# Two matmuls instead of three per weight tile in the SwiGLUs of a hybrid encoder trunk, in groups of eight, and 1/rms of their norm later

## The chip, the cores and the metric

One core of one Trainium2 chip runs the whole program in one launch. The metric is the device time of an execution in microseconds; the figure of a kernel is the median of its runs.

## The reference, cut to what is computed

Two layers over 256 tokens of width 1024 in float32, each with two SwiGLU half-steps around a mixer, then a gated per-layer input:

```python
for i in range(DEPTH):                                   # 2
    x = x + 0.5 * swiglu(rmsnorm(x, g_ffa[i]), ...)      # silu(h @ w_gate) * (h @ w_up) @ w_down, 1024 -> 2816 -> 1024
    u = rmsnorm(x, g_mix[i]) @ w_in[i]                   # neighbourhood attention and Hyena convolution on its columns
    ...
    x = x + 0.5 * swiglu(rmsnorm(x, g_ffb[i]), ...)
    x = x + sigmoid(rmsnorm(x, g_ple[i]) @ w_ple_gate[i]) * (p[i] @ w_ple_proj[i])
return rmsnorm(x, g_final)
```

## The kernel before, in words

Activations lie turned: features on the 128 partitions, the 256 tokens (T) along the row. `x` is eight such blocks. A float32 product is made from rounded parts: every operand is split into a high part (fp32r, the rounded value) and a low part (the rest), and `mm3` (L164) issues three TensorE matmuls for each 128x128 weight tile: high weight on high input (L165), high weight on low input (L166), low weight on high input (L167), all of 256 columns, into the same 256 columns of a PSUM bank. A bank holds 512 float32 per partition, and there are eight (`bank`, L99).

Weights come as a stream of 1 MB pieces of 16 tiles (`load`, L213; three buffers), and are split in halves of 8 tiles by `part` (L234): ScalarE casts the high part (L250), VectorE subtracts for the low part (L253; in the mixer every third one on GpSimd). Six halves are held; when half n is begun, `refill` (L270) lets the split of half n + 5 be issued.

The norm's gain is folded in ahead: `prep` (L327) makes the two parts of g * x (ScalarE L329, VectorE L331), which lie beside one another in one tile of 512 columns, and adds up the squares (ScalarE L314, GpSimd L317). 1/rms is found later by `Rstd` (L365): two small TensorE matmuls per 128 tokens (L379), Newton steps on VectorE, and two matmuls that spread it over all partitions into `rb` (L403 to L405). Its place is set in steps: STAT_F = 8 (STAT0 = 6 in the very first) and SPREAD_AT = 7. The products don't wait for it; the work behind them multiplies by `rb`.

TensorE and ScalarE run in the order in which the program issues their work; the order on VectorE and GpSimd is planned by the framework. The products set the pace: after every three weight tiles (TICK) `tick` lets each live piece of side work ("fiber") issue one step, up to its next `yield`. `finish` makes a fiber issue all that is left before a product that reads its result.

A SwiGLU (`ffn`, L425) first makes four products (gate and up of two blocks of 128 hidden features) together, block of x by block of x, then for each further block of features (22 in all) gate and up into the two halves of one bank. `gated` (L431) multiplies both by `rb` in one VectorE instruction of 512 columns (L439), takes Silu on ScalarE (L442), multiplies (VectorE, L445) and splits the result (L447, L449). The down projection then makes 8 columns of blocks from 22 tiles each, and adds half of each to x (L480). Beside the first SwiGLU of each layer `filter_steps` (L491) computes the Hyena filter's spectrum, on all engines; after the SwiGLUs come the mixer (L611) and the gated input (`ple`).

Of the kernel before, what the change touches and what calls it, by code (L numbers as in the profile page):

```python
# [28 lines left out]
HALF = 8  # L29

# [6 lines left out]
STAT0 = 6  # L37
# [11 lines left out]
SPREAD_AT = 7  # L49
FILTER = 10  # L50
# [9 lines left out]
# columns of the packed per-partition parameters of one layer  # L60
# [15 lines left out]
def hybrid_trunk(ctx: ExitStack, tc: tile.TileContext, w, xT, pT, rpb, small, wf, zT, dft, idft, decay, out):  # L76
# [8 lines left out]
    k1 = ctx.enter_context(tc.tile_pool(name="k1", bufs=12))  # L85
# [33 lines left out]
    class Fiber:  # L119
        """Work of several engines, emitted step by step between the products."""  # L120
# [43 lines left out]
    def mm3(o, lh, ll, rh, rl, start, stop):  # L164
        PE.matmul(o, lh, rh, start=start, stop=False)  # L165
        PE.matmul(o, lh, rl, start=False, stop=False)  # L166
        PE.matmul(o, ll, rh, start=False, stop=stop)  # L167
        if not Pace.inside:
            Pace.total += 1
            Pace.count += o.free_size() // T if hasattr(o, "free_size") else o.shape[-1] // T  # L170
            while Pace.count >= TICK:
                Pace.count -= TICK
                tick()

# [21 lines left out]
    # even times, odd times, and the latter's negative; real and imaginary parts  # L196
# [37 lines left out]
    def part(steps=1):  # L234
        """The next 8 weight tiles in their two 12-bit parts."""
# [25 lines left out]
    def half():  # L261
        """The two parts of the next 8 weight tiles."""
        n = Stream.used
        Stream.used += 1
        h, l, fb = Stream.ready.pop(n)
        fb.finish()
        refill(n - LAG)
        return h, l

    def refill(done):  # L270
        """Halves up to `done` - 1 are used up: others take their place."""
        while Stream.parted < min(done + WBUFS, 2 * DEPTH * PIECES):
            Pace.live.insert(0, part())

    class Tiles:
        """Weight tiles one after the other."""
# [16 lines left out]
    class Inputs:  # L293
        """The two parts of g * x of the norm at hand."""
# [5 lines left out]
        def __getitem__(self, c):  # L300
            hl, fb = self.xs[c]
            fb.finish()
            return hl[:, :T], hl[:, T:]

    class Squares:
        """Sum of the squares of `n` blocks, in whatever order they come."""
# [27 lines left out]
    def onward(i, cg, c, before):  # L334
        """After `before`, which brings x[c] up to date, the next norm's input."""
# [9 lines left out]
    def rsqrt(v):  # L345
        """v ** -0.5 of two columns by Newton's steps from the exponent's halving."""
# [18 lines left out]
    class Rstd:  # L365
        """1/rms of each token: `r`, tokens on partitions, and `dst`, on all partitions."""
# [45 lines left out]
    def norm(xs, at):  # L412
        return Rstd(rb, Norm.sq.parts, D, [fb for _, fb in xs.xs] + early, at)
# [11 lines left out]
    def ffn(i, cg_next, i_next):  # L425
# [3 lines left out]
        rs = norm(xs, STAT0 if Stream.used == 0 else STAT_F)  # L429

        def gated(pg, pu, joint, hl):  # L431
            yield from rest(EV)
            yield from rs.wait()
            gu = t2(s="gu")
            if joint is None:
                V.tensor_mul(gu[:, :T], pg, rb)
                V.tensor_mul(gu[:, T:], pu, rb)
            else:
                V.tensor_tensor(v2(gu), v2(joint), rb2(), op=ALU.mult)  # L439
            yield  # L440
            s = t1()
            S.activation(s, gu[:, :T], AF.Silu)  # L442
            yield
            a = t1()
            V.tensor_mul(a, s, gu[:, T:])  # L445
            yield
            S.copy(hl[:, :T], a)  # L447
            yield
            V.tensor_sub(hl[:, T:], a, f(hl[:, :T]))  # L449

        def start(*a):
            hl = t2(F32R, "act")
            act.append((hl, spawn(gated(*a, hl))))

        heads = [bank()[:, :T] for _ in range(4)]
        for c in range(KD):
            xh, xl = xs[c]
            for o in heads:
                wh, wl = ws.next()
                mm3(o, wh, wl, xh, xl, c == 0, c == KD - 1)  # L460
        for j in (0, 2):
            start(heads[j], heads[j + 1], None)
        for ff in range(2, NF):
            b = bank()
            for o in (b[:, :T], b[:, T:]):
                product(o, ws, xs)
            start(None, None, b)
        ws = Tiles()
        new_norm()
        for c in range(KD):  # L470
            ps = bank()[:, :T]
            for k in range(NF):
                wh, wl = ws.next()
                hl, fb = act[k]
                fb.finish()
                mm3(ps, wh, wl, hl[:, :T], hl[:, T:], k == 0, k == NF - 1)

            def half_step(c=c, ps=ps):
                yield from rest(EV)
                V.scalar_tensor_tensor(x[c], ps, 0.5, x[c], op0=ALU.mult, op1=ALU.add)  # L480

            onward(i_next, cg_next, c, half_step())

    def stacked(src, h):
        """From values that lie on both halves of the partitions: high parts on one, low parts on the other."""
# [5 lines left out]
    def filter_steps(i):  # L491
# [96 lines left out]
        # sums and differences of the even and the odd times' spectra  # L588
# [22 lines left out]
    def mixer(i):  # L611
# [3 lines left out]
        def columns(between=None):  # L615
            """Two blocks of 128 columns of u from the next 16 weight tiles."""
# [7 lines left out]
        # values, tokens on partitions  # L624
# [36 lines left out]
        class QK:  # L661
            """Queries and keys of a pair of heads, the queries with zeros for the other head."""
# [25 lines left out]
        class Head:  # L688
            """One head's probabilities: the scores' softmax, then turned over."""
# [56 lines left out]
        def head_norm(src, sq, ch, hl):  # L746
            """The two parts of g * y, and its squares added up."""
# [21 lines left out]
        def conv(b, chans, res):  # L769
            """Short convolution of the two blocks of channels in a bank."""  # L770
# [66 lines left out]
        def spectral(a, ps):  # L837
            """The gated input's spectrum, frequencies on partitions, times the filter's."""
# [257 lines left out]
def _rpb_index():  # L1096
    """Where the bias of (token of the query, token of the key) lies; the last place outside the window."""
# [7 lines left out]
def _tiles(wm):  # L1105
    """[K, M] -> [M tiles, K tiles, 128, 128]."""
# [4 lines left out]
def _weights(a):  # L1111
# [9 lines left out]
    def swiglu(i, s):  # L1121
# [4 lines left out]
        put(_tiles(a[f"w_ff{s}_down"][i]))  # L1126
# [77 lines left out]
```

## Time and profile before

| | |
|---|---|
| runs of the kernel | 1114.73, 1115.2, 1116.72 us (median 1115.2) |
| span of the profiled execution | 1112.9 us, first to last instruction |
| what lies around the span | 2.3 us, taken as the median of the runs less the span (the profiled execution's own total is not given apart from its span) |
| instructions in the span | 21462, of them 8828 matmuls and as many weight loads |
| HBM read | 191.86 MB, 173 GB/s over the span |
| mean granted TensorE clock | 0.996 of full speed |

The rows give busy time per engine, instructions by line, waits and times of start. PE is TensorE, PEld its weight loads, DVE VectorE, ACT ScalarE, POOL GpSimd. Starts are from the beginning of the span. Matmuls overlap in the pipeline, so their listed durations are longer than the distance from one start to the next.

### The profile page before, as it was taken

To read this page: it belongs to the slowest core of one execution; us is meant where nothing else is said; L and a number is where in the kernel's file an instruction comes from. 1 tells how busy PE (TensorE), PEld (TensorE's weight loads), DVE (VectorE), ACT (ScalarE), POOL (GpSimd) and SP (SyncE) were. 2 spreads that over 40 slices of the span, in tenths; PEclk is the share of its full clock that TensorE was granted. 3 is DMA by queue.
4 is the path that set the end of the run, shared out by engine and by line. 5 is a ranking of instruction groups with operands and counts; after the bars stand their busy time and mean duration, and the time that the engine had idled before them with its cause. 6 is when DMAs were issued, how large, how long until landed. Compare 5 with 4: busy or idle time off the path is not lost.

```text
span 1112.9 us, 21462 instructions
## 1 busy us (share of the span) xinstructions
PE 1087.2 (98%) x8828; PEld 1074.4 (97%) x8828; DVE 840.5 (76%) x1352; ACT 600.3 (54%) x1006; POOL 205.1 (18%) x182
## 2 busy tenths in 40 slices
PE   7999999999999999999999999999999999999996
PEld 7999999999999999999999999999989999999995
DVE  4988777798999766655878878677899986665554
ACT  6555455376746444444655455544855554444444
POOL 3000111544362000011100002125433700000111
PEclk9999999999999999999999999999999999999998
DMA  8565455454335555455455554454523464555421
GB/s 319 215 236 201 154 191 186 170 173 169 114 117 197 190 189 190 176 175 183 161 195 200 215 188 174 173 185 152 190 77 114 142 217 183 189 189 186 176 95 39
DMA packets 32994, 194.29 MB, mean 175 GB/s; under 512 B 3584, under 2 KB 6528, under 8 KB 10880
## 3 DMA queue, kind: packets, MB, share of 16 engines
q1 hardware_dynamic: 32896, 192.92, 48.4%
q8 instruction: 69, 1.13, 0.4%
q14 instruction: 29, 0.24, 0.1%
HBM read 191.86 MB, written 1.05 MB: 173 GB/s over the span
## 4 chain that ended last, share of the span: by engine, by line
PE 80%; DVE 11%; ACT 4%; issue 3%; DMA 1%; POOL 1%; SPq 0%; ACTq 0%; DVEq 0%; POOLq 0%
PE ps L166 26%; PE ps L167 26%; PE ps L165 26%; DVE wl L253 2%; ACT wh L250 2%; DMA raw<-in_w 1%; DVE rt L360 1%; DVE s L783 1%; DVE s L886 1%; DVE x L887 1%; ACT t L723 1%; DVE xg L331 0%; POOL acc L317 0%; ACT t L716 0%; DVE y L752 0%
## 5 line engine op out<-in xcount | busy, mean ns | idle before, releaser
L253 DVE TENSOR_TENSOR wl<-raw,wh 128x1024 fp32r<-128x1024 f32 (+1 forms) x328 | 410.9, 1257 | 193.7 <-ACT wh L250 191.7
L250 ACT CAST wh<-raw 128x1024 fp32r<-128x1024 f32 (+1 forms) x350 | 362.0, 1040 | 321.6 <-PE ps L166 226.8
L165 PE MATMUL ps<-xg,wh 128*128 128x256 f32 x1856 | 528.2, 285 | 5.9 <-ACT xg L1032 5.9
L166 PE MATMUL ps<-xg,wh 128*128 128x256 f32 x1856 | 527.5, 284 | 5.4 <-DVE xg L331 5.3
L167 PE MATMUL ps<-xg,wl 128*128 128x256 f32 x1856 | 526.9, 284 | 0.0
L166 PEld LDWEIGHTS ps<-xg,wh 128*128 128x128 f32 x1856 | 357.7, 193 | 7.2 <-DVE xg L331 6.3
L165 PEld LDWEIGHTS ps<-xg,wh 128*128 128x128 f32 x1856 | 357.8, 193 | 6.3 <-ACT xg L1032 5.9
L167 PEld LDWEIGHTS ps<-xg,wl 128*128 128x128 f32 x1856 | 357.7, 193 | 0.0
L167 PE MATMUL ps<-act,wl 128*128 128x256 f32 x704 | 199.4, 283 | 0.0
L165 PE MATMUL ps<-act,wh 128*128 128x256 f32 x704 | 199.4, 283 | 0.0
L166 PE MATMUL ps<-act,wh 128*128 128x256 f32 x704 | 199.4, 283 | 0.0
L317 POOL TENSOR_TENSOR acc<-acc,q 128x256 f32<-128x256 f32 x62 | 65.9, 1064 | 541.2 <-ACT q L314 524.8
L165 PEld LDWEIGHTS ps<-act,wh 128*128 128x128 f32 x704 | 135.2, 192 | 0.4
L166 PEld LDWEIGHTS ps<-act,wh 128*128 128x128 f32 x704 | 135.2, 192 | 0.4
L167 PEld LDWEIGHTS ps<-act,wl 128*128 128x128 f32 x704 | 135.2, 192 | 0.0
L439 DVE TENSOR_TENSOR gu<-ps,rb 128x512 f32<-128x512 f32 x80 | 55.0, 689 | 20.6 <-PE ps L167 19.0
L253 POOL TENSOR_TENSOR wl<-raw,wh 128x1024 fp32r<-128x1024 f32 x22 | 55.0, 2499 | 62.7 <-ACT wh L250 49.9
L566 POOL TENSOR_TENSOR t<-t,t 128x512 f32<-128x512 f32 x4 | 5.7, 1414 | 225.7 <-PE ps L167 121.0
L329 ACT ACTIVATE xg<-x,sm 128x256 fp32r<-128x256 f32 x56 | 28.1, 506 | 33.2 <-DVE x L480 14.0
L397 ACT ACTIVATE s<-ident,rl 128x128 fp32r<-128x128 f32 x24 | 8.3, 395 | 65.4 <-DVE rl L392 65.4
L442 ACT ACTIVATE s<-gu 128x256 f32<-128x256 f32 x88 | 35.9, 414 | 12.8 <-DVE gu L439 12.0
L449 DVE TENSOR_TENSOR act<-s,act 128x256 fp32r<-128x256 f32 x88 | 38.3, 444 | 0.0
(193 smaller groups left out, 1222.7 us busy)
## 6 DMA issues: line engine op xcount, KB each, us to landing
raw<-in_w SPq DMA_DIRECT2D x172, 1024.0 KB, 4.8
bias<-in_rpb SPq DMA_DIRECT2D x16, 256.0 KB, 2.8
raw<-in_w SPq DMA_DIRECT2D x4, 256.0 KB, 4.6
x<-in_xT SPq DMA_DIRECT2D x8, 128.0 KB, 4.8
raw<-in_w SPq DMA_DIRECT2D x2, 512.0 KB, 5.7
t<-in_wf SPq DMA_DIRECT2D x4, 256.0 KB, 5.4
dec<-in_decay SPq DMA_DIRECT2D x4, 256.0 KB, 5.4
out<-o SPq DMA_DIRECT2D x4, 256.0 KB, 2.4
```

The costliest lines, as they stand in the source:

```text
L165: PE.matmul(o, lh, rh, start=start, stop=False)
L166: PE.matmul(o, lh, rl, start=False, stop=False)
L167: PE.matmul(o, ll, rh, start=False, stop=stop)
L250: S.copy(h[:, a : a + k], src)
L253: e.tensor_sub(l[:, a : a + k], src, f(h[:, a : a + k]))
L317: G.tensor_add(self.ac, self.ac, q)
L329: S.activation(hl[:, :T], x[c], AF.Copy, scale=g)
L360: V.tensor_scalar(r[:, c], y[:, c], y[:, c], hv[:, c], op0=ALU.mult, op1=ALU.mult)
L439: V.tensor_tensor(v2(gu), v2(joint), rb2(), op=ALU.mult)
L442: S.activation(s, gu[:, :T], AF.Silu)
L449: V.tensor_sub(hl[:, T:], a, f(hl[:, :T]))
L723: S.activation(e[:, cs], e[:, cs], AF.Copy, scale=ri[:, tt : tt + 1])
```

## The change

In the SwiGLUs alone, a weight tile's high part is multiplied with the high and low parts of the input in one matmul of 512 columns, since both parts lie side by side. It fills a whole bank: the first 256 columns hold high x high, the second 256 high x low. The third matmul (low weight on high input, 256 columns) adds to the second half. Eight wide ones are issued first and then the eight narrow ones that belong to them (fewer at the end of a product). The two halves of the bank are added afterwards: ScalarE copies the second half to a small buffer, VectorE adds the first. A gate and an up product now take a bank each and are evicted without waiting for 1/rms; gate is multiplied by it on VectorE and up on GpSimd. The half-step after the down projection becomes two additions. The first two columns of the down projection are made for features 0 to 15 first and then for 16 to 21, with the weights laid out in that order on the host. The first norm of the program loses its own STAT0, the SwiGLU norms spread 1/rms 10 steps later instead of 7, and there are 15 small buffers instead of 12. The mixer and the gated input keep `mm3`. Comments taken out and a helper split off `mm3` without effect on the order are left out below.

```diff
+GROUP = 8
-STAT0 = 6
+SPREAD_F = 10
+DOWN = [(c, k) for ks in (range(16), range(16, NF)) for c in range(2) for k in ks]
+DOWN += [(c, k) for c in range(2, KD) for k in range(NF)]
...
-    k1 = ctx.enter_context(tc.tile_pool(name="k1", bufs=12))
+    k1 = ctx.enter_context(tc.tile_pool(name="k1", bufs=15))
...
+    class Wide:
+        later = []
+        @classmethod
+        def mm(cls, b, lh, ll, r, start, stop):
+            PE.matmul(b, lh, r, start=start, stop=False)
+            cls.later.append((b[:, T:], ll, r[:, :T], stop))
+            if stop or len(cls.later) == GROUP:
+                cls.flush()
+            paced()
+        @classmethod
+        def flush(cls):
+            for o, ll, rh, stop in cls.later:
+                PE.matmul(o, ll, rh, start=False, stop=stop)
+            cls.later.clear()
+
+    def summed(dst, b):
+        S.copy(dst, b[:, T:])
+        yield
+        yield
+        V.tensor_add(dst, dst, b[:, :T])
...
+    def product2(b, ws, xs):
+        for c in range(KD):
+            wh, wl = ws.next()
+            Wide.mm(b, wh, wl, xs.both(c), c == 0, c == KD - 1)
...
     def ffn(i, cg_next, i_next):
...
-        rs = norm(xs, STAT0 if Stream.used == 0 else STAT_F)
-        def gated(pg, pu, joint, hl):
-            yield from rest(EV)
-            yield from rs.wait()
-            gu = t2(s="gu")
-            ...
-                V.tensor_tensor(v2(gu), v2(joint), rb2(), op=ALU.mult)
-            yield
-            s = t1()
-            S.activation(s, gu[:, :T], AF.Silu)
-            ...
+        rs = norm(xs, STAT_F, SPREAD_F)
+        def taken(b):
+            dst = t1(s="gu")
+            def go():
+                yield from rest(EV)
+                yield from summed(dst, b)
+            return dst, spawn(go())
+        def gated(gate, up, hl):
+            (g, gf), (u, uf) = gate, up
+            while not (gf.done and uf.done):
+                yield
+            yield from rs.wait()
+            V.tensor_mul(g, g, rb)
+            G.tensor_mul(u, u, rb)
+            yield
+            yield
+            s = t1()
+            S.activation(s, g, AF.Silu)
+            yield
+            yield
+            V.tensor_mul(s, s, u)
+            yield
+            yield
+            S.copy(hl[:, :T], s)
+            yield
+            V.tensor_sub(hl[:, T:], s, f(hl[:, :T]))
...
-        for c in range(KD):
-            ps = bank()[:, :T]
-            for k in range(NF):
-                wh, wl = ws.next()
-                hl, fb = act[k]
-                fb.finish()
-                mm3(ps, wh, wl, hl[:, :T], hl[:, T:], k == 0, k == NF - 1)
+        def half_step(c, ps):
+            yield from rest(EV)
+            for b in (ps[:, :T], ps[:, T:]):
+                V.scalar_tensor_tensor(x[c], b, 0.5, x[c], op0=ALU.mult, op1=ALU.add)
+        out = {}
+        for c, k in DOWN:
+            if k == 0:
+                out[c] = bank()
+            wh, wl = ws.next()
+            hl, fb = act[k]
+            fb.finish()
+            Wide.mm(out[c], wh, wl, hl, k == 0, k == NF - 1)
+            if k == NF - 1:
+                onward(i_next, cg_next, c, half_step(c, out.pop(c)))
...
-        put(_tiles(a[f"w_ff{s}_down"][i]))
+        put(_tiles(a[f"w_ff{s}_down"][i])[tuple(np.array(DOWN).T)])
```

## Rows read from the trace of the kernel before

**Rows 1.** The page: its head, section 1 (busy us, share of the span, instructions by engine) and the head of section 4, the chain of work that ended last.

```profile
span 1112.9 us, 21462 instructions
...
PE 1087.2 (98%) x8828; PEld 1074.4 (97%) x8828; DVE 840.5 (76%) x1352; ACT 600.3 (54%) x1006; POOL 205.1 (18%) x182
...
PE 80%; DVE 11%; ACT 4%; issue 3%; DMA 1%; POOL 1%; SPq 0%; ACTq 0%; DVEq 0%; POOLq 0%
```

**Rows 2.** The timeline of TensorE from 59.8 to 64.0 us, gate and up products of the first SwiGLU: start, duration, engine, line, operation, tiles, shapes. The 34 rows between these two are alike, in the order L166, L167, L165.

```profile
59.76 0.28 PE L165 MATMUL ps<-xg,wh 128*128 128x256 f32 x1
...
63.96 0.28 PE L167 MATMUL ps<-xg,wl 128*128 128x256 f32 x1
```

**Rows 3.** Busy time by stretch: from:to and length, then busy us (and instructions) of TensorE, its weight loads, VectorE, ScalarE, GpSimd, granted clock, DMA share, GB/s. The first three and the last three lie beside the filter in the first SwiGLUs of the two layers, 400 to 466 is gate/up without it and 466 to 530 a down projection.

```profile
30.00:70.00 40.00, 40.00 (x336) 40.00 (x335) 36.66 (x70) 23.80 (x41) 0.00 (x0) 1.00 0.63 226
70.00:100.00 30.00, 30.00 (x253) 30.00 (x252) 25.20 (x44) 15.93 (x26) 0.00 (x0) 1.00 0.63 227
100.00:136.00 36.00, 36.00 (x296) 35.65 (x295) 27.58 (x38) 17.09 (x25) 3.46 (x2) 1.00 0.48 176
400.00:466.00 66.00, 66.00 (x552) 66.00 (x551) 43.30 (x58) 31.29 (x46) 0.00 (x0) 1.00 0.49 179
466.00:530.00 64.00, 64.00 (x536) 64.00 (x535) 35.51 (x40) 30.61 (x41) 7.97 (x7) 1.00 0.52 185
536.00:575.00 39.00, 39.00 (x327) 39.00 (x327) 33.19 (x63) 25.10 (x45) 6.87 (x7) 1.00 0.55 198
575.00:620.00 45.00, 45.00 (x377) 45.00 (x376) 38.52 (x65) 26.71 (x43) 0.00 (x0) 1.00 0.53 188
620.00:667.00 47.00, 47.00 (x392) 46.91 (x391) 35.38 (x54) 24.38 (x40) 0.00 (x0) 1.00 0.56 202
```

**Rows 4.** Groups by line, all of the span: TensorE's low-weight matmuls on the norm's output (xg) and on the gated activation (act); count, then busy us, mean ns, idle before.

```profile
L167 PE MATMUL ps<-xg,wl 128*128 128x256 f32 x1856 | 526.9, 284 | 0.0
L167 PE MATMUL ps<-act,wl 128*128 128x256 f32 x704 | 199.4, 283 | 0.0
```

**Rows 5.** The timeline of TensorE from 205.8 to 219.5 us. At 205.77 the first matmul of 512 columns follows ones of 256, 206.24 is the third, 207.16 the seventh and 207.61 the ninth; from 207.16 to 214.41 there are 33 of them in a row, both counted. Four one-column matmuls stand at 214.64; from 215.32 to 217.41 there are ten. At 218.55 the first of 256 columns follows, and 219.50 is the ninth.

```profile
205.77 0.40 PE L165 MATMUL ps<-t,dft_h 128*128 128x512 f32 x1
...
206.24 0.39 PE L167 MATMUL ps<-t,dft_l 128*128 128x512 f32 x1
...
207.16 0.39 PE L165 MATMUL ps<-wh,xg 128*128 128x512 f32 x1
...
207.61 0.39 PE L167 MATMUL ps<-wh,xg 128*128 128x512 f32 x1
...
214.41 0.39 PE L167 MATMUL ps<-wh,xg 128*128 128x512 f32 x1
...
215.32 0.40 PE L166 MATMUL ps<-wl,xg 128*128 128x512 f32 x1
...
217.41 0.39 PE L166 MATMUL ps<-wl,xg 128*128 128x512 f32 x1
...
218.55 0.28 PE L165 MATMUL ps<-xg,wh 128*128 128x256 f32 x1
...
219.50 0.28 PE L167 MATMUL ps<-xg,wl 128*128 128x256 f32 x1
```

**Rows 6.** Instructions of single lines: count, then duration in ns least/median/most, first and last start in us, shapes.

```profile
L439 DVE TENSOR_TENSOR gu<-ps,rb x80: 677/692/693, 39.5 to 1006.0; 128x512 f32<-128x512 f32 x80
L445 DVE TENSOR_TENSOR s<-s,gu x88: 407/418/422, 42.1 to 1008.2; 128x256 f32<-128x256 f32 x88
L480 DVE SCALAR_TENSOR_TENSOR x<-ps,x x32: 362/424/425, 148.9 to 1069.4; 128x256 f32<-128x256 f32 x32
L442 ACT ACTIVATE s<-gu x88: 399/414/421, 40.3 to 1006.9; 128x256 f32<-128x256 f32 x88
L976 ACT COPY t<-ps x8: 576/583/587, 526.6 to 1076.0; 128x512 f32<-128x512 f32 x8
```

**Rows 7.** GpSimd's additions of two 128x256 blocks and VectorE beside them: L317 and L331 over the span (ns least/median/most), L317 in the first norm alone (0 to 40 us), its group on the page (count, busy us, mean ns, idle before), and the timeline around 495 us on the two engines.

```profile
L317 POOL TENSOR_TENSOR acc<-acc,q x62: 722/990/1812, 19.2 to 1101.3; 128x256 f32<-128x256 f32 x62
L331 DVE SCALAR_TENSOR_TENSOR xg<-x,sm,xg x56: 471/482/1030, 151.7 to 1071.9; 128x256 fp32r<-128x256 f32 x56
L317 POOL TENSOR_TENSOR acc<-acc,q x7: 722/739/1784, 19.2 to 26.6; 128x256 f32<-128x256 f32 x7
L317 POOL TENSOR_TENSOR acc<-acc,q 128x256 f32<-128x256 f32 x62 | 65.9, 1064 | 541.2 <-ACT q L314 524.8
...
494.46 1.23 DVE L253 TENSOR_TENSOR wl<-raw,wh 128x1024 fp32r<-128x1024 f32 x1 [0.58 <-ACT wh L250]
495.60 0.96 DVE L331 SCALAR_TENSOR_TENSOR xg<-x,sm,xg 128x256 fp32r<-128x256 f32 x1
495.29 0.99 POOL L317 TENSOR_TENSOR acc<-acc,q 128x256 f32<-128x256 f32 x1 [4.77 <-ACT q L314]
```

**Rows 8.** The timeline where TensorE stands: the first two matmuls of the program, the first norm's sum, and the start of the second SwiGLU. In brackets the idle time before and what ended it.

```profile
5.92 0.58 PE L165 MATMUL ps<-xg,wh 128*128 128x256 f32 x1 [5.92 <-ACT xg L1032]
...
6.64 0.58 PE L166 MATMUL ps<-xg,wh 128*128 128x256 f32 x1
...
27.41 0.61 PE L379 MATMUL ps<-onesf,acc 128*128 128x1 f32 x4 [0.80 <-POOL acc L317]
...
340.30 0.39 PE L166 MATMUL ps<-xg,wh 128*128 128x256 f32 x1 [1.26 <-DVE xg L331]
```

More of the change, by code (lines that the diff above doesn't have):

```diff
@@ L167, in mm3, with paced @@
         PE.matmul(o, ll, rh, start=False, stop=stop)
+        paced(o.free_size() // T if hasattr(o, "free_size") else o.shape[-1] // T)
+    def paced(n=1):
         if not Pace.inside:
             Pace.total += 1
-            Pace.count += o.free_size() // T if hasattr(o, "free_size") else o.shape[-1] // T
+            Pace.count += n
             while Pace.count >= TICK:
@@ L300, in __getitem__, with both @@
         def __getitem__(self, c):
+            hl = self.both(c)
+            return hl[:, :T], hl[:, T:]
+        def both(self, c):
             hl, fb = self.xs[c]
             fb.finish()
-            return hl[:, :T], hl[:, T:]
+            return hl
     class Squares:
@@ L410, in wait, with norm @@
                 yield
-    def norm(xs, at):
-        return Rstd(rb, Norm.sq.parts, D, [fb for _, fb in xs.xs] + early, at)
+    def norm(xs, at, spread=SPREAD_AT):
+        return Rstd(rb, Norm.sq.parts, D, [fb for _, fb in xs.xs] + early, at, spread)
     def rb2():
@@ L440, in gated @@
+        def gated(gate, up, hl):
+            (g, gf), (u, uf) = gate, up
+            while not (gf.done and uf.done):
+                yield
+            yield from rs.wait()
+            V.tensor_mul(g, g, rb)
+            G.tensor_mul(u, u, rb)
+            yield
             yield
             s = t1()
-            S.activation(s, gu[:, :T], AF.Silu)
+            S.activation(s, g, AF.Silu)
             yield
-            a = t1()
-            V.tensor_mul(a, s, gu[:, T:])
             yield
-            S.copy(hl[:, :T], a)
+            V.tensor_mul(s, s, u)
@@ L448, in gated, with start @@
             yield
-            V.tensor_sub(hl[:, T:], a, f(hl[:, :T]))
-        def start(*a):
+            yield
+            S.copy(hl[:, :T], s)
+            yield
+            V.tensor_sub(hl[:, T:], s, f(hl[:, :T]))
+        def start(gate, up):
             hl = t2(F32R, "act")
-            act.append((hl, spawn(gated(*a, hl))))
-        heads = [bank()[:, :T] for _ in range(4)]
+            act.append((hl, spawn(gated(gate, up, hl))))
+        heads = [bank() for _ in range(4)]
         for c in range(KD):
-            xh, xl = xs[c]
-            for o in heads:
+            for b in heads:
@@ L459, in ffn @@
                 wh, wl = ws.next()
-                mm3(o, wh, wl, xh, xl, c == 0, c == KD - 1)
-        for j in (0, 2):
-            start(heads[j], heads[j + 1], None)
+                Wide.mm(b, wh, wl, xs.both(c), c == 0, c == KD - 1)
+        heads = [taken(b) for b in heads]
+        start(*heads[:2])
+        start(*heads[2:])
         for ff in range(2, NF):
[L464 to L467, printed above, removed]
+            pair = []
+            for _ in range(2):
+                b = bank()
+                product2(b, ws, xs)
+                pair.append(taken(b))
+            start(*pair)
@@ L468, in ffn @@
         ws = Tiles()
         new_norm()
-        for c in range(KD):
-            ps = bank()[:, :T]
-            for k in range(NF):
-                wh, wl = ws.next()
-                hl, fb = act[k]
-                fb.finish()
-                mm3(ps, wh, wl, hl[:, :T], hl[:, T:], k == 0, k == NF - 1)
[L478 to L482, printed above, removed]
+        def half_step(c, ps):
+            yield from rest(EV)
+            for b in (ps[:, :T], ps[:, T:]):
+                V.scalar_tensor_tensor(x[c], b, 0.5, x[c], op0=ALU.mult, op1=ALU.add)
```

4 lines of the change are left out of this document (removed).

## The prediction

> **What bounds the kernel now.** I read the page first. TensorE's matmuls are busy for 1087.2 of 1112.9 us, VectorE for 840.5, ScalarE and GpSimd far less, and 80% of the chain that ended last is TensorE [rows 1]. The page says itself that a busy TensorE is not TensorE at its peak, because matmuls overlap. So the next view is the order in time, where the number to read is the distance from start to start. In a stretch of gate and up products 35 such distances of 256-column matmuls take 63.96 - 59.76 = 4.20 us, 120.0 ns each [rows 2], although one matmul is listed at 280 ns. The granted clock is 1.00 there [rows 3], which is 2.4 GHz, so the 256 columns alone are 256 / 2.4 = 106.7 ns and 13.3 ns come on top of every matmul. That is the quantity that this change works on. The count of stalls is small: matmuls stand at this distance nearly everywhere. The second engine to watch is VectorE: 36.66 us of 40 at 30 to 70 us, where the Hyena filter runs beside the first SwiGLU, but 43.30 of 66 in a gate/up stage without the filter [rows 3].
>
> **TensorE.** Each SwiGLU weight tile now takes three 256-column matmuls; it will take one of 512 and one of 256. Columns stay at 768, instructions fall from three to two. The number of tiles is 1408 gate/up and 704 down, 2112 in all (704 is in the row; 1408 is 4 SwiGLUs x 44 x 8 by the loops, the other 448 of 1856 being mixer and last projection) [rows 4]. The trace has both sizes, with the same 128 x 128 weights. In a long run of 512-column matmuls the distance is (214.41 - 207.16) / 32 = 226.6 ns, again 13.3 ns above the columns' 213.3 [rows 5]. So a tile in steady state goes from 3 x 120.0 = 360.0 to 226.6 + 120.0 = 346.6 ns, 13.4 ns less; 2112 tiles give 28.3 us. That is the upper end.
>
> The switch from narrow to wide isn't free. After 256-column work the first eight wide ones take 207.61 - 205.77 = 1.84 us, 27 ns more than eight steady ones, and after the wide run eight narrow ones take 219.50 - 218.55 = 0.95 us, 10 ns less than steady [rows 5]. So one group of eight and eight costs about 17 ns over steady. By the code a SwiGLU has 7 groups in its first four products, 40 in the other gate/up products and 24 in the down projection: 71, and 284 in all, 4.8 us. Net gain 28.3 - 4.8 = **23.5 us**. For the lower end I take the wide matmuls that follow four one-column ones: (217.41 - 215.32) / 9 = 232 ns [rows 5], which leaves 8 ns a tile, 16.9 us. I take the middle row, because it is the one that follows 256-column work.
>
> The Trainium skill ("TensorE: Matmul & The Clock Gate", section "Back-to-back issue gap") gives N / 2.4 plus only 2.5 ns. By that one matmul less per tile would be worth 2112 x 2.5 ns, an estimate of 5.3 us. The trace doesn't agree: it has 13.3 ns at both sizes.
>
> **VectorE and GpSimd.** Per gate/up pair (16 tiles, 5.76 us now) VectorE loses the 692 ns multiplication by 1/rms out of PSUM and gains two additions from PSUM and one multiplication, each like the 418 ns of L445 or the 424 ns of L480, the one that reads PSUM [rows 6]. That is 3 x 0.42 - 0.69 = +0.57 us. GpSimd gains one 128x256 multiplication of two SBUF operands. Its like, L317, has 722 / 990 / 1812 ns (least, median, most) [rows 7]. It can slow VectorE: beside the GpSimd addition at 495.29 us, VectorE's L331 took 0.96 us, and the addition itself 0.99 while a weight split ran [rows 7]. L331 takes 0.48 us at its median, so the price there is 0.48 us. The price of one multiplication to VectorE lies between 0 (it falls on additions that read PSUM, or on idle time) and 0.74 (VectorE stands for the whole of an undisturbed L317, whose median in the first norm, while VectorE had little to do, is 739 ns [rows 7]). I take 0.4, near the one clean pair, since part of them will fall on PSUM work.
>
> So a pair costs VectorE 0.97 us more. Without the filter (400 to 466 us, 11.5 pairs of 3.78 us [rows 3]) that is 4.75 us of the new 16 x 0.349 = 5.58, 85%: nothing on the path. With it, 30 to 70 us holds 6.94 pairs: 36.66 + 6.7 = 43.4 us of work in 38.8 us of new time, 4.6 behind; 70 to 100 adds 1.1; 100 to 136 gives 1.3 back. In the second layer 536 to 575 and 575 to 620 fall behind by 1.8 and 2.4, 620 to 667 recovers 2.3 [rows 3]. What covers this is the stock of parted weights: six half-pieces of 8 tiles, so five ahead, 40 tiles or 14 us. A lag of 5.7 us stays inside it. If the cover were gone, these some 10 us would stand on the path. I book 1.5 us for moments in which VectorE also waits for another engine.
>
> **Work that I cost at nothing.** ScalarE gets 176 copies out of PSUM, 0.41 us each by L442 (at most the 0.58 of L976, a copy of 512 out of PSUM): 31.29 of 66 us become about 41, still free [rows 3, 6]. The second half-step addition per down column is 8 x 0.42 = 3.4 us per down stage, on a VectorE that has 35.51 of 64 there [rows 3, 6]. The longer chain from product to activation (one copy, two GpSimd or VectorE steps more, about 3.6 us) is covered by the new order of the down projection: pairs 16 to 21 are first read after 32 tiles, 11 us, against 16 to 21 tiles now. PSUM is let go earlier than now, since a product no longer waits in its bank for 1/rms; the 1/rms itself is known some 80 tiles into a SwiGLU, by when ten evicted blocks wait in the fifteen small buffers; if they ran out, ScalarE would stand until then, at most one product (2.8 us) each time. DMAs are the same in number and size; only the order of the down tiles in memory differs.
>
> **Edges.** The wait of 0.80 us before the first norm's matmul (its sum of squares is late on GpSimd [rows 8]) should go, as this matmul is put two steps, 6 tiles, later: -1.0 with the pause of the queue around it. The first matmul will need both parts of its input, so it starts at about 6.6 instead of 5.92 us, where one narrow matmul ran alone: +0.5. Where a SwiGLU follows the mixer, TensorE waits for the low part of the input, 1.26 us at 340 us [rows 8]. In groups of eight the blocks are needed in pairs, so earlier by half a pair: +0.75 in each layer, +1.5.
>
> **Sum.** -23.5 - 1.0 + 0.5 + 1.5 + 1.5 = -21.0 us. The profiled execution's span is 1112.9 us, 2.3 below the median of the runs, which holds what lies around the span; nothing in the change touches that. From the median: 1115.2 - 21 = **1094 us**. About 0.2%, or 2 us, is what a measurement of this kernel can tell from no change.
>
> **Rivals.** First, *wide matmuls never settle in groups of eight*: they all stay at the (206.24 - 205.77) / 2 = 235 ns of the first two after a switch [rows 5], and the narrow ones at 120. Then a tile saves 5 ns, 10.6 us, and with the other terms it is 1115.2 - 10.6 + 2.5 = 1107 us. For it: the first entries after every switch are slow, and there are 284 switches. Against it: the eight as a whole took 1.84 us, so they do settle. The 2.5 ns of the Trainium skill, named above, would give 1115.2 - 5.3 + 2.5 = 1112 by the same road: little saved per instruction.
>
> Second, on the other side, *VectorE becomes the pace beside the filter*. Its place is 30 to 136 and 536 to 667 us, its price what GpSimd's multiplication takes from VectorE. If it is the whole 1.06 us of a mean L317 [rows 7], the two stretches hold 89.4 + 18.4 x 1.63 = 119.4 and 107.1 + 22.7 x 1.63 = 144.1 us of VectorE work against 102.7 and 127.0 us of TensorE's, 34 us too much; without the stock of weights that gives 1115.2 - 22.5 + 34 = 1127 us, slower. It decides from about 0.8 us a multiplication, where the excess eats the 22.5. For it: 92% busy in the first stretch already, and some L317 take up to 1.8 us. Against it: the clean pair shows 0.48, and the stock of 14 us hides the first part.
>
> The Trainium skill ("SBUF — State Buffer", section on the shared port pair) says that a two-input VectorE operation and a GpSimd operation that reads SBUF exclude each other for a whole instruction. The trace agrees (0.96 for 0.48 us beside GpSimd); by that rule alone the price could reach 0.74, close to the point that decides.
>
> Third, *the change is absorbed*: stalls of the two kinds together eat the gain, and it ends within 2 us of before.
>
> **Chances.** Forecast 0.72 (1086, if all 28.3 us come and no stall, to 1104, if 16.9 us come and 6 us of stalls). First rival 0.12, 1104 to 1112. Second 0.11. Third 0.05. The range 1086 to 1110 leaves out the second and third and the end of the first. Faster: 0.72 and nearly all of the first, 0.83; same 0.06; slower 0.11.
>
> **What would show it.** Right: some 2112 fewer matmuls and weight loads; wide distances of 227 to 236 and narrow ones of 113 to 120 ns in the SwiGLUs; the gate/up stage of the first SwiGLU shorter by about 3%, and the mixer as long as now; VectorE around 900 us busy without long waits of TensorE for `wl`. Wrong: TensorE waiting for `wl` or for a PSUM bank at 30 to 136 us, VectorE full there, L331 and L253 well above their present means; or wide distances of 235 throughout.

## The result and the profile after

| | before | after |
|---|---|---|
| median of the runs | 1114.97 us (1114.7 to 1116.72) | 1100.17 us (1098.25 to 1101.02) |
| span of the profiled execution | 1112.9 us | 1099.0 us |

The ratio is 0.9861 with a 95% interval of 0.9847 to 0.9875: 14.8 us less, where 21 were forecast. The four runs of the kernel after lie 2.8 us apart, the shortest at a mean granted clock of 0.997 and the longest at 0.993. The page of the kernel after (head, and section 1), against [rows 1]:

```profile
span 1099.0 us, 17994 instructions
...
PE 1069.0 (97%) x6716; PEld 964.8 (88%) x6716; DVE 895.5 (81%) x1552; ACT 645.6 (59%) x1182; POOL 306.8 (28%) x270
```

8828 - 6716 = 2112 matmuls and as many weight loads are gone, as counted. VectorE (DVE) is 55 us busier, GpSimd (POOL) 102. The timeline of TensorE in a gate/up stage without the filter, against [rows 2, 5] (start, duration, engine, line; L191 is the wide matmul, L200 the narrow one, merged where they follow one another):

```profile
419.89 2.00 PE L191 MATMUL ps<-xg,wh 128*128 128x512 f32 x8
421.73 1.11 PE L200 MATMUL ps<-xg,wl 128*128 128x256 f32 x8
422.69 2.00 PE L191 MATMUL ps<-xg,wh 128*128 128x512 f32 x8
424.53 1.12 PE L200 MATMUL ps<-xg,wl 128*128 128x256 f32 x8
425.48 0.86 PE L191 MATMUL ps<-xg,wh 128*128 128x512 f32 x3
```

Two groups take 425.48 - 419.89 = 5.59 us, 349.4 ns a tile where it was 360.0; eight wide ones take 1.84 us and eight narrow ones 0.95 to 0.96, the very sums of [rows 5]. So TensorE's term came as worked out. To see where the rest went I took the stages apart, by the start of the first matmul that reads `act` (down projection) and the first one behind it that reads `xg` (next stage); lengths in us. Each column is one profiled execution of its kernel; the edits e1 to e9 are explained below:

```
stage                                         before    after   e1      e2      e3      e6      e8      e9
SwiGLU 1 of layer 1, gate/up (with filter)    134.23   134.57  134.07  131.10  129.84  132.35  130.54  130.22
  its down projection (filter's end)           67.01    65.15   65.15   65.83   65.60   65.14   65.14   65.60
mixer and SwiGLU 2, gate/up                   254.42   253.08  254.76  251.40  251.84  252.28  252.22  251.11
  its down projection                          69.12    67.25   67.25   66.76   67.26   67.25   67.25   66.75
gated input, SwiGLU 1 of layer 2, gate/up     153.62   150.02  153.63  151.31  149.55  150.03  150.03  149.56
  its down projection (filter's end)           67.02    65.15   65.14   65.84   65.60   65.14   65.14   65.60
mixer and SwiGLU 2, gate/up                   254.50   252.43  255.42  252.47  252.45  253.64  253.61  251.24
  its down projection                          69.12    67.25   67.26   66.76   67.25   67.26   67.26   66.76
```

Each down projection got 1.87 us shorter, 176 tiles by 10.6 ns. At that rate each gate/up stage (352 tiles) should have lost 3.7 us. The third did (3.60), the fourth lost 2.07, the second 1.34, and the first, beside the filter, became 0.34 us longer. Busy time by stretch, columns as in [rows 3], after:

```profile
20.00:46.00 26.00, 26.00 (x151) 22.80 (x150) 18.32 (x38) 15.97 (x32) 8.29 (x9) 1.00 0.72 255
46.00:66.00 20.00, 20.00 (x118) 17.64 (x117) 20.00 (x39) 10.96 (x23) 7.67 (x6) 1.00 0.47 166
66.00:71.00 5.00, 1.99 (x13) 1.51 (x12) 4.13 (x9) 4.51 (x9) 1.32 (x1) 1.00 0.78 262
...
71.00:74.40 3.40, 3.40 (x14) 2.91 (x13) 3.40 (x6) 2.30 (x6) 1.65 (x1) 0.50 0.57 152
...
340.00:344.00 4.00, 3.77 (x14) 3.34 (x15) 4.00 (x5) 4.00 (x7) 3.17 (x3) 0.58 0.22 47
```

VectorE is busy for 20.00 of 20 us from 46 to 66 us; before it was 18.68 (the second row is for later):

```profile
46.00:66.00 20.00, 20.00 (x170) 20.00 (x168) 18.68 (x34) 12.11 (x21) 0.00 (x0) 1.00 0.63 224
...
340.00:344.00 4.00, 2.85 (x21) 2.65 (x22) 4.00 (x5) 4.00 (x7) 3.22 (x3) 1.00 0.29 55
```

Then TensorE stands. The timeline of the three engines after, 66 to 71 us; L562 is a matmul of the Hyena filter, L546 the VectorE split that it reads, L573, L576 and L544 earlier steps of the same chain, and in brackets the idle time and what ended it:

```profile
66.63 0.63 PE L191 MATMUL ps<-xg,wh 128*128 128x512 f32 x2
70.27 0.39 PE L562 MATMUL ps<-s,t 128*128 128x256 f32 x1 [3.01 <-DVE s L546]
...
66.11 0.28 DVE L573 TENSOR_SCALAR s<-s 128x256 f32<-128x256 f32 x1
...
67.87 1.22 DVE L288 TENSOR_TENSOR wl<-raw,wh 128x1024 fp32r<-128x1024 f32 x1 [0.81 <-ACT wh L285]
...
69.80 0.42 DVE L546 TENSOR_TENSOR s<-s,s 64x256 fp32r<-64x256 f32 x1
...
66.49 0.42 ACT L576 ACTIVATE s<-s 128x256 f32<-128x256 f32 x1 [3.89 <-DVE s L573]
66.81 1.03 ACT L285 CAST wh<-raw 128x1024 fp32r<-128x1024 f32 x1
...
68.32 0.40 ACT L544 CAST s<-s 128x256 fp32r<-128x256 f32 x1
```

ScalarE waits 3.89 us for VectorE, its weight cast stands behind that wait, VectorE then waits for the cast, and TensorE, whose order is fixed, waits 3.01 us for the filter. The split's input was ready at 68.72 us (end of L544), but it began at 69.80: 1.1 us of the wait it stood behind other work on VectorE. After that TensorE's granted clock was 0.50 from 71.0 to 74.4 us, its lower level of 1.2 GHz. The second such place is the SwiGLU after the mixer (timeline after, against the last line of [rows 8]):

```profile
337.22 1.09 PE L191 MATMUL ps<-xg,wh 128*128 128x512 f32 x4
340.24 1.75 PE L191 MATMUL ps<-xg,wh 128*128 128x512 f32 x4 [1.92 <-DVE xg L370]
341.79 1.91 PE L200 MATMUL ps<-xg,wl 128*128 128x256 f32 x8
```

One wait of 1.92 us, and a clock of 0.58 over 340 to 344; before, the waits there came in smaller pieces and the clock was 1.00. A third place lies ahead of it, inside the mixer, which the change leaves alone. Its first matmul starts at 205.92 us after and at 207.16 before [rows 5], and a later one of its matmuls starts at the same time in both kernels, after first and before second:

```profile
205.92 0.39 PE L170 MATMUL ps<-wh,xg 128*128 128x512 f32 x1
...
236.11 0.39 PE L170 MATMUL ps<-s,t 128*128 128x256 f32 x1 [0.62 <-ACT t L740]
```

```profile
236.19 0.38 PE L165 MATMUL ps<-s,t 128*128 128x256 f32 x1
```

So the mixer took 1.16 us longer to get there (30.19 for 29.03 us): TensorE came sooner, and the chain on ScalarE and VectorE that it waits for did not. In the second layer the same stretch took 29.83 us for 28.91.

### The profile page after: what moved, and what is told of

Its sections match the earlier page's. It is cut to its first block, busy times and chain, and to the rows that moved or that the text cites. A ratio compares the mean times of both kernels' runs of the same rounds, so it can differ in the third digit from the quotient of the medians.

```text
span 1099.0 us, 17994 instructions
## 1 busy us (share of the span) xinstructions
PE 1069.0 (97%) x6716; PEld 964.8 (88%) x6716; DVE 895.5 (81%) x1552; ACT 645.6 (59%) x1182; POOL 306.8 (28%) x270
## 4 chain that ended last, share of the span: by engine, by line
PE 80%; DVE 11%; ACT 4%; issue 3%; DMA 1%; POOL 0%; SPq 0%; DVEq 0%; ACTq 0%; POOLq 0%
PE ps L191 43%; PE ps L200 23%; PE ps L171 4%; PE ps L172 4%; PE ps L170 4%; DVE wl L288 2%; ACT wh L285 1%; DVE rt L399 1%; DVE s L841 1%; DVE x L945 1%; DVE s L944 1%; ACT t L781 1%; DMA t<-in_idft 1%; DVE xg L370 0%; DMA raw<-in_w 0%
## 5 line engine op out<-in xcount | busy, mean ns | idle before, releaser
L288 DVE TENSOR_TENSOR wl<-raw,wh 128x1024 fp32r<-128x1024 f32 (+1 forms) x328 | 416.3, 1272 | 135.1 <-ACT wh L285 113.3
L191 PE MATMUL ps<-xg,wh 128*128 128x512 f32 x1408 | 363.2, 396 | 12.3 <-DVE xg L1093 6.6
L191 PEld LDWEIGHTS ps<-xg,wh 128*128 128x128 f32 x1408 | 254.6, 191 | 59.4 <-DVE xg L370 7.5
L200 PEld LDWEIGHTS ps<-xg,wl 128*128 128x128 f32 x1408 | 195.4, 193 | 14.1
L200 PE MATMUL ps<-xg,wl 128*128 128x256 f32 x1408 | 200.5, 284 | 0.0
L490 POOL TENSOR_TENSOR gu<-gu,rb 128x256 f32<-128x256 f32 x88 | 94.8, 1082 | 368.1 <-DVE gu L208 288.0
L191 PE MATMUL ps<-act,wh 128*128 128x512 f32 x704 | 179.0, 392 | 0.0
L191 PEld LDWEIGHTS ps<-act,wh 128*128 128x128 f32 x704 | 126.3, 189 | 22.1
L170 PE MATMUL ps<-xg,wh 128*128 128x256 f32 x448 | 127.5, 285 | 0.0
L172 PE MATMUL ps<-xg,wl 128*128 128x256 f32 x448 | 126.7, 283 | 0.0
L171 PE MATMUL ps<-xg,wh 128*128 128x256 f32 x448 | 126.7, 283 | 0.0
L200 PEld LDWEIGHTS ps<-act,wl 128*128 128x128 f32 x704 | 97.1, 190 | 7.6
L200 PE MATMUL ps<-act,wl 128*128 128x256 f32 x704 | 99.4, 282 | 0.0
L171 PEld LDWEIGHTS ps<-xg,wh 128*128 128x128 f32 x448 | 85.9, 192 | 0.1
L170 PEld LDWEIGHTS ps<-xg,wh 128*128 128x128 f32 x448 | 85.9, 192 | 0.1
L172 PEld LDWEIGHTS ps<-xg,wl 128*128 128x128 f32 x448 | 85.9, 192 | 0.0
L288 POOL TENSOR_TENSOR wl<-raw,wh 128x1024 fp32r<-128x1024 f32 x22 | 55.9, 2540 | 63.7 <-ACT wh L285 50.9
L208 DVE TENSOR_TENSOR gu<-gu,ps 128x256 f32<-128x256 f32 x176 | 71.9, 412 | 0.1
```

Of the source, the lines that this page charges most:

```text
L191: PE.matmul(b, lh, r, start=start, stop=False)
L208: V.tensor_add(dst, dst, b[:, :T])
L288: e.tensor_sub(l[:, a : a + k], src, f(h[:, a : a + k]))
L490: G.tensor_mul(u, u, rb)
```

## The experiments

Theory A: the pair of matmuls saves what the prediction says everywhere; what is missing was lost to TensorE's waits in gate/up stages, where VectorE is late, and to the half clock behind them. Theory B: the switch between wide and narrow eats the gain.

**e1, the down projection alone.**

```diff
-                mm3(ps, wh, wl, hl[:, :T], hl[:, T:], k == 0, k == NF - 1)
+                Wide.mm(ps, wh, wl, hl, k == 0, k == NF - 1)
...
-                V.scalar_tensor_tensor(x[c], ps, 0.5, x[c], op0=ALU.mult, op1=ALU.add)
+                for b in (ps[:, :T], ps[:, T:]):
+                    V.scalar_tensor_tensor(x[c], b, 0.5, x[c], op0=ALU.mult, op1=ALU.add)
```

> The kernel before with wide and narrow matmuls in groups of eight in the down projections alone (old order of their tiles), gate and up as before. Theory A (a tile saves 13.4 ns of TensorE less 17 ns per group, and nothing in the down stage stands in the way; what the whole change lost against the forecast was lost in gate/up): four down stages get 1.9 us shorter each, so 1115.0 - 7.5 = 1107.5 us, between 1106 and 1109. Theory B (wide matmuls stay at 235 ns in short groups): 5 ns a tile, 704 tiles, 1115.0 - 3.5 = 1111.5 us.

Measured: 1108.6 us, ratio 0.9947 (0.9932 to 0.9962). The four down stages are as short as in the whole change (65.15 and 67.25 us), 7.5 us together, and the old gate/up stages kept their lengths within 0.35 us but for the fourth (0.9 us longer, nearly all of it in the mixer, ahead of the second layer's counterpart of the matmul shown above). Theory A holds for the down projection.

**e2, groups of one.**

```diff
-GROUP = 8
+GROUP = 1
```

> The changed kernel with groups of one: each wide matmul is followed by its narrow one. If every switch from narrow to wide costs 27 ns and gives 10 back (as the sum of the prediction has it), 2112 - 284 more switches cost 17 ns each: 31 us, 1131 us. If only the first wide ones after a long narrow run are slow (a store that fills), a pair takes 233 + 116 = 349 ns as now in a group: 1100 us within 2 us. In between, the cost per switch is the excess over 1100 divided by 1828.

Measured: 1098.43 us, ratio 0.9858 (0.9843 to 0.9872), the same as in groups of eight within the intervals. The 17 ns a switch that the prediction took from a long run don't add up: theory B falls, and so does my sum for many switches. The timeline of TensorE in e2, at 420 us and at 90 us:

```profile
419.83 0.39 PE L191 MATMUL ps<-xg,wh 128*128 128x512 f32 x1
420.06 0.27 PE L200 MATMUL ps<-xg,wl 128*128 128x256 f32 x1
...
421.91 0.39 PE L191 MATMUL ps<-xg,wh 128*128 128x512 f32 x1
```

```profile
89.88 0.40 PE L191 MATMUL ps<-xg,wh 128*128 128x512 f32 x1
90.11 0.28 PE L200 MATMUL ps<-xg,wl 128*128 128x256 f32 x1
...
92.00 0.40 PE L191 MATMUL ps<-xg,wh 128*128 128x512 f32 x1
```

Six pairs take 2.08 us at 420 and 2.12 at 90: 346.7 ns, the steady sum with no switch cost at all, against 353.3. The table shows the same: the down projections of the second SwiGLUs get shorter than with groups of eight (66.76 for 67.25), those of the first longer (65.83 for 65.15). What sets the pace I don't know. The first stage got 3.5 us shorter (131.10), and in it the filter's matmul waits for 0.18 us only, although neither the filter nor the work on VectorE was touched:

```profile
68.11 0.39 PE L562 MATMUL ps<-s,t 128*128 128x256 f32 x1 [0.18 <-DVE s L546]
```

So the groups' size matters for that wait too; how, no run shows.

**e3, more time for the filter's split.**

```diff
-FILTER = 10
+FILTER = 7
...
-            yield from rest(FR)
+            yield from rest(FR + 4)
```

The second place is the pause between the split of a filter layer's output and the next layer's matmul.

> The changed kernel with 4 more steps between the filter's split of a layer's output on VectorE and the matmul that reads it (three places), and 7 instead of 10 steps at the filter's other pauses, so that it ends at about the same place. Theory A (VectorE lags some 7 us behind TensorE's order at 60 to 70 us, and this reaches TensorE not by the weights but by the filter's matmul, which stood 3.0 us at 67 us and then cost a stretch at half clock): that wait goes, the first SwiGLU's gate/up stage gets 4 to 4.6 us shorter, 1095.6 to 1096.5 us. Rival (VectorE is simply full; the lag comes back as waits for weight parts): 1099 to 1101 us, with TensorE waiting for wl before 136 us.

Measured: 1097.8 us, ratio 0.9852 (0.9835 to 0.9868), by the total not separable from the change. Theory A's total (at most 1096.5) was missed. By the stage it was right: 134.57 to 129.84 us, 4.7 less (0.45 of it came back in the down projection), and no wait for weights came in its place. The filter's matmul still waits, for 1.15 us:

```profile
68.50 0.36 PE L562 MATMUL ps<-s,t 128*128 128x256 f32 x1 [1.15 <-DVE s L546]
```

The second stage got 1.2 us shorter. The stretch of the mixer shown above takes 28.92 us here, as short as before the change:

```profile
201.90 0.39 PE L170 MATMUL ps<-wh,xg 128*128 128x512 f32 x1
...
230.82 0.39 PE L170 MATMUL ps<-s,t 128*128 128x256 f32 x1
```

**e4, up times 1/rms on VectorE.**

```diff
-            G.tensor_mul(u, u, rb)
+            V.tensor_mul(u, u, rb)
```

> The changed kernel with the multiplication of up by 1/rms on VectorE instead of GpSimd: VectorE gets 0.42 us more per pair and loses what GpSimd takes from it now (about 0.2 us on average). Theory A (VectorE's total is what counts beside the filter): 0.2 us a pair more, the lag grows by 2 to 4 us in the first SwiGLU of each layer, 1101 to 1105 us. Rival (GpSimd's hold on VectorE makes it late): 1096 to 1099 us.

Measured: 1099.91 us, ratio 0.9865 (0.9851 to 0.9880): neither expectation, no change. Section 1 of its page says why:

```profile
PE 1068.3 (97%) x6716; PEld 964.8 (88%) x6716; DVE 906.0 (82%) x1640; ACT 645.7 (59%) x1182; POOL 212.0 (19%) x182
```

VectorE has 88 instructions more and is only 906.0 - 895.5 = 10.5 us busier. By themselves they would have made it some 30 us busier, an estimate: such an instruction is listed at 0.41 us, but four in a row start a third of a us apart (kernel after; two more lie between these):

```profile
62.97 0.41 DVE L208 TENSOR_TENSOR gu<-gu,ps 128x256 f32<-128x256 f32 x1
...
63.97 0.41 DVE L572 SCALAR_TENSOR_TENSOR s<-s,s 128x256 f32<-128x256 f32 x1
```

So GpSimd's multiplications had held VectorE for about 19 us, some 0.2 us each. The mean lengths of VectorE's groups give the same: L489, which multiplies gate while GpSimd multiplies up, gets shorter (after, then e4; count, then busy us, mean ns, idle before):

```profile
L489 DVE TENSOR_TENSOR gu<-gu,rb 128x256 f32<-128x256 f32 x88 | 45.7, 529 | 2.3 <-ACT rb L444 2.2
```

```profile
L489 DVE TENSOR_TENSOR gu<-gu,rb 128x256 f32<-128x256 f32 x88 | 37.7, 428 | 2.2 <-ACT rb L444 2.2
```

With L288 (328 of them, 1272 to 1252 ns) and L502 (88, 473 to 438 ns) this comes to 18.5 us. Handing the multiplications to GpSimd saved VectorE 0.12 us apiece. The first stage was 132.87 us, 1.7 shorter and not longer, and the wait at L562 2.30 us: without GpSimd's hold most of that wait stays.

**e5, the first four products in groups of four.**

```diff
         for c in range(KD):
             for b in heads:
                 wh, wl = ws.next()
                 Wide.mm(b, wh, wl, xs.both(c), c == 0, c == KD - 1)
+            Wide.flush()
```

> The changed kernel, but in each SwiGLU's first four products the narrow matmuls follow after four wide ones, so that a block of x is needed only when the one before is used up (groups of four there). Theory A (in the SwiGLU after the mixer TensorE stood 1.92 us in one piece at 338 us and then ran some 3 us at half clock, because a group of eight asks for two blocks at once): the wait is cut into pieces as in the kernel before, the clock stays up, that SwiGLU's gate/up stage gets 1 to 2 us shorter; 1098 to 1099 us. Rival (that stage is bound by the arrival of the last block from VectorE, whatever the order): 1100 us, and the stage from 205.9 to 459.0 us as long as now.

Measured: 1099.58 us, ratio 0.9865 (0.9851 to 0.9880). Its timeline at the second SwiGLU, and 340 to 344 us by stretch; then the same place in e8 (below), where the groups of eight stay as they were:

```profile
339.50 1.19 PE L191 MATMUL ps<-xg,wh 128*128 128x512 f32 x4 [1.45 <-DVE xg L370]
...
342.05 1.20 PE L191 MATMUL ps<-xg,wh 128*128 128x512 f32 x4 [0.88 <-DVE xg L370]
```

```profile
340.00:344.00 4.00, 3.12 (x19) 2.56 (x18) 4.00 (x5) 3.58 (x5) 2.43 (x3) 1.00 0.46 133
```

```profile
336.23 1.20 PE L191 MATMUL ps<-xg,wh 128*128 128x512 f32 x4 [1.92 <-DVE xg L370]
...
338.78 0.96 PE L191 MATMUL ps<-xg,wh 128*128 128x512 f32 x3 [0.41 <-DVE xg L370]
```

```profile
336.00:340.00 4.00, 3.36 (x17) 2.77 (x18) 4.00 (x5) 4.00 (x7) 3.17 (x3) 1.00 0.26 53
```

The wait is cut in two, the clock stays at 1.00, and the stage (253.08 us after) became 252.24, 0.8 us shorter and not 1 to 2. But e8 has the wait of 1.92 us in one piece, and its clock stays at 1.00 and its stage is as short (252.22), as it is in e6 (1.93 us, 252.28). In both e5 and e8 the two waits make 2.33 us. So cutting the wait gained nothing that shows: TensorE waits until VectorE hands over the blocks of x, as the rival said, and the 0.8 us go with the half clock, which came behind this wait in the kernel after and not in e6 and e8. The 3 us at 67 us are still there.

**e6, 1/rms as early as before** (as in the program's first norm before; in the other SwiGLU norms the 6 is two steps earlier than there).

```diff
-STAT_F = 8
-SPREAD_F = 10
+STAT_F = 6
+SPREAD_F = 7
```

> The changed kernel with 1/rms of the SwiGLU norms as early as in the kernel before (6 and 7 steps instead of 8 and 10). VectorE had 18.3 us of work from 20 to 46 us and 20.0 of 20 from 46 to 66. Theory A1 (the later 1/rms moves the work of the waiting pairs into the filter's time and so makes part of the lag of the first SwiGLU): the wait of 3.0 us at 67 us shrinks to about 1 and its half-clock stretch goes, 1097 us, less the 1 us of the norm's sum that is late again, so 1097 to 1098. Rival A2 (the lag comes from the added work alone): 1100 to 1101 us.

Measured: 1100.3 us, ratio 0.9864 (0.9847 to 0.9880). By the total it is A2's number, but the waits moved. L562 starts at 70.22 without a wait of note. In its place TensorE stands twice earlier, for the sum of squares (L418) and for the spreading (L442):

```profile
27.41 0.61 PE L418 MATMUL ps<-onesf,acc 128*128 128x1 f32 x4 [1.50 <-POOL acc L356]
36.43 0.35 PE L442 MATMUL ps<-s,ones 128*128 128x256 f32 x1 [1.54 <-DVE s L435]
```

The split that L562 reads was made at the same time as in the kernel after:

```profile
69.75 0.42 DVE L546 TENSOR_TENSOR s<-s,s 64x256 fp32r<-64x256 f32 x1
```

There it began at 69.80. So VectorE was not sooner; TensorE came 3 us later, having stood that long before. Whether the later 1/rms has a part in VectorE's lag (A1) this run doesn't show. What it shows is that the later place takes away some 3 us of waits, and that about as much stands at 67 us.

**e7, groups of one and the filter's pauses.** The edits of e2 and e3 together.

> Groups of one together with the filter's longer pauses (the two edits that gained alone). If they gain in different places (the filter's wait at 67 us, and the SwiGLU after the mixer, where groups of one ask for one block at a time), gate/up of the first SwiGLU is about 129.5 to 131 us, the next stage about 251 us: 1095 to 1097 us. If both only removed the same wait at 67 us: 1098 us.

Measured: 1096.95 us, ratio 0.9838 (0.9823 to 0.9853). As expected of edits that gain in different places, though the first stage (130.21 us) gained no more than in e3.

**e8, gate not multiplied by 1/rms.**

```diff
-            V.tensor_mul(g, g, rb)
```

> The changed kernel without the multiplication of gate by 1/rms on VectorE (88 instructions of 0.42 us left out, so the activations are scaled wrongly). Nothing else in the filter or on TensorE is touched. Theory A (VectorE's lag makes the filter's matmul late): nine pairs lie between 46 and 67 us, 3.8 us less work there, so the wait of 3.0 us at 67 us and the half clock behind it go: gate/up of the first SwiGLU 130 us, in all 1095 to 1096 us. Rival (the filter's matmul is late for its own chain of ScalarE and VectorE, not for VectorE's load): 1099 to 1100 us.

Measured: 1097.83 us, ratio 0.984 (0.9826 to 0.9855); the stage is 130.54 us, 4.0 less, at an untouched filter, and the wait at 67 us is down to

```profile
67.76 0.39 PE L561 MATMUL ps<-s,t 128*128 128x256 f32 x1 [0.45 <-DVE s L545]
```

So VectorE's load makes the wait, and not the filter's own chain alone. The total gained 2.3 us, less than the 4 expected: the fourth stage took 1.2 back. In this execution the clock was 0.50 there for 3.3 us, behind a wait of 1.19 us inside the mixer; the kernel after has the same wait (1.20 us) and kept 1.00:

```profile
814.20 1.92 PE L787 MATMUL ps<-ident,t 128*128 128x128 f32 x8 [1.19 <-ACT t L780]
```

```profile
816.30:819.60 3.30, 3.30 (x18) 3.30 (x17) 3.30 (x6) 3.30 (x10) 1.02 (x1) 0.50 0.00 0
```

**e9 and e10, the better version.** e9 has e3's pauses, groups of eight in the first SwiGLU of each layer and of one in the second; e10 has the pauses and groups of two (last two lines of the diff).

```diff
-            if stop or len(cls.later) == GROUP:
+            if stop or len(cls.later) == cls.group:
...
+        Wide.group = GROUP
         flt = spawn(filter_steps(i))
         ffn(i, C_MIX, i)
...
+        Wide.group = 1
         ffn(i, C_PLE, i)
...
-GROUP = 8
+GROUP = 2
```

> The filter's longer pauses, groups of eight in the first SwiGLU of each layer and groups of one in the second. With groups of one the pair of matmuls took 346.7 ns in the second SwiGLUs and 353.4 in the first, with groups of eight 349.7 in both. If that belongs to the SwiGLU and not to chance: against the longer pauses alone (span 1094.7) each second SwiGLU gains 0.5 us in its down projection and some 1 us in gate/up, and the wait after the mixer is cut into pieces without a half-clock stretch (1 us in the first layer): span 1091 to 1092, median 1094 to 1095.5 us. If the two paces come and go by chance: 1096 to 1098 us.

> The filter's longer pauses and groups of two throughout. If what counts is how many wide matmuls stand in a row after a narrow one (the first two of a run took 234 ns each in the kernel before, the narrow ones after two wide 116 and 113), four take 697 ns, 348.5 a pair: 2112 times 1.2 ns less than groups of eight, 2.5 us: 1095 to 1096 us. If the slower pace of groups of one (353.4) comes back with more switches: 1098 to 1101 us.

Measured: e9 1093.8 us, ratio 0.9820 (0.9805 to 0.9836), beyond the interval of the change (0.9847 to 0.9875); e10 1095.4 us, ratio 0.9827 (0.9809 to 0.9845). Both came as expected. In e9 the second SwiGLUs ran at the pace of 346.7 ns again (their down projections took 66.75 and 66.76 us), so the two paces aren't chance. e9 has the lowest median of this study; from e10 its interval doesn't separate it.

## Why the prediction was right or wrong

The forecast of 1094 us was 6 us too low; the direction was right, and 14.8 of the 21 us came.

- **TensorE, -23.5 us.** The mechanism and the size were right: 10.6 ns a tile measured in all four down projections, 22.4 us if every stage had it, from the distances of [rows 2, 5]. The 2.5 ns a matmul of the Trainium skill ("TensorE: Matmul & The Clock Gate", "Back-to-back issue gap", there for an isolated matmul) would have given an estimated 5.3 us; the matmul that is gone was worth 10.6 ns here. The term inside it, 17 ns for each switch, holds for groups of eight and is no cost per switch (e2, e9).
- **First rival** (wide ones stay at 235 ns): fell; eight took 1.84 us.
- **VectorE's load.** The price of GpSimd's multiplication, 0.4 us in the sum, measured about 0.2 (e4). It is below the 0.74 to which the rule of the Trainium skill ("SBUF — State Buffer", on the shared port pair) leads; that GpSimd's work holds VectorE, as the rule has it, shows. The other part of the 0.97 us a pair was too large as well: I added up listed lengths, and VectorE's instructions overlap as the matmuls do. The terms make 88 x 0.97 + 32 x 0.42 = 98.8 us; VectorE got 55.0 us busier. The "around 900 us" among the signs of being right came true (895.5), but not by these terms, which lead to 939: that was luck.
- **The step that failed is the cover over VectorE's lag.** I let the stock of five half-pieces of weights hide it, booking 1.5 us. The weights did hide it: TensorE waited for no `wl`. But the filter's own matmul stands in TensorE's fixed order a few steps behind its VectorE split, with no stock at all, and the lag came through there although VectorE's added work was half of what I had booked: 3.01 us and a stretch at half clock, some 4 us by e3 and e8. I priced the queue of weights and left out the other reader of VectorE. That groups of one shrink the same wait to 0.18 us (e2) I can't explain.
- **Second rival** (VectorE becomes the pace beside the filter): true at one place for some 4 us, not over the stretch.
- **The mixer, "as long as now".** It was 1.2 us longer in the first layer and 0.9 in the second, a term that I put at nothing: its matmuls wait for a chain on ScalarE and VectorE that didn't get sooner when TensorE did. In the first layer the 1.2 us went with the filter's other pauses (e3). In the second e1 has the same 0.9 us with the down projections changed alone, and no run took it away. What makes the chain late is open.
- **Edges.** The wait for the first norm's sum went, as booked; in e6 the earlier place cost 3 us of waits. The first matmul started at 6.20 us (6.6 forecast). After the mixer I booked 0.75 us per layer. The stages gained 2.4 (second) and 1.6 us (fourth) less than 3.7; without the mixer's part 1.2 and 0.7 are left, and about 0.8 of the 1.2 is the half clock, which e6 and e8 don't have there. So the 0.75 was near in the second layer and too much in the first.
- **Work costed at nothing** (copies on ScalarE, the second half-step addition, the longer chain to the activations, PSUM, the small buffers): no wait of TensorE names any of it. Whether the second half-step addition, which lies just ahead of the mixer, has a part in the mixer's wait is open.

The sum by stages, in us of span: 22.4 from the tiles, less 0.3 at the start, less 4.1 in the first stage, 2.1 in the two mixers, 2.0 in the SwiGLUs behind them and 0.1 in the third stage, comes to the 13.9 within rounding.

## What to carry to other kernels

Take the worth of a matmul that goes away from the distance between starts at both sizes, not from listed durations: that sum came true within a nanosecond a tile. Do the same for an engine off the path: VectorE's instructions overlap here too. When an engine off the path is driven near full, list every reader of it in the critical engine's fixed order and give each its own cover; a deep stock for one of them says nothing about the others. And handing work to an engine that shares something with the loaded one saves less than its length: measure what the loaded engine gets back. Before one execution's stage is compared with another's, look at the granted clock of both: here a stretch at half clock made and unmade 0.8 to 1.2 us.

## What the runs showed of the hardware that I had not expected

- Alternating wide and narrow matmuls one by one runs at 346.7 ns a pair in the second SwiGLU of a layer and mostly at 353 in the first (e2, e7), though instructions, shapes and granted clock (1.00) are alike; groups of eight ran at 349 to 350 in both. The cause is open.
- A stretch of 3.4 us at a granted clock of 0.50 followed single waits of TensorE of 3.01 and 1.92 us in the kernel after, and a wait of 1.19 us in e8. Behind a wait of 1.92 us in e8 and one of 1.20 us in the kernel after, each at the same place in the program, the clock stayed at 1.00. So the length of the wait alone doesn't decide; what does is open.
